# Gates of a PEER layer: float32 one-hots from one VectorE instruction, and one float32 product a token

## The chip, the cores and the metric

One Trainium2 chip, one core of it. The metric is the device time of one execution in microseconds (us): the median of several runs. Engines in the profile: PE is TensorE (PEld its weight loads), DVE is VectorE, ACT is ScalarE, POOL is GpSimd, SP is SyncE, which issues most of the DMAs.

## The reference

Two layers (`DEPTH = 2`) on 512 tokens of width 1024. Each layer is a token mixer (four heads of differential attention and eight heads of stick-breaking attention) and then PEER, a retrieval over 128² = 16384 experts of one neuron each; a residual with a factor and a layer norm follow each half. The part that matters here:

```python
q = (xt @ w_query).reshape(T, PEER_HEADS, 2, HALF_Q)
scores = einsum('thpc,hpnc->thpn', q, sub_keys)
top_s, top_i = top_k(scores, 16)
cand_s = top_s[:, :, 0, :, None] + top_s[:, :, 1, None, :]
cand_i = top_i[:, :, 0, :, None] * 128 + top_i[:, :, 1, None, :]
best_s, best_pos = top_k(cand_s, 16)
idx = take_along_axis(cand_i, best_pos)      # 8 heads x 16 = 128 experts a token
gate = softmax(best_s)
...
act = gelu(einsum('cd,ced->ce', x, expert_u[idx]))
y = einsum('ce,ced->cd', gate * act, expert_v[idx])
```

## The kernel before

The 512 tokens are four blocks of 128. PEER is done in two ways at once. For blocks 0 and 1 (`BLK_A`) the rows of the chosen experts are gathered: in each layer and block 128 rows of `u` and 128 of `v`, each by an indirect DMA that GpSimd issues (line 624), into one of five buffers named `row`, and each used by one VectorE instruction of 128x1024 (line 634 for `u`, line 645 for `v`). For blocks 2 and 3 (`BLK_B`) the function `dense` multiplies with all 16384 experts in 32 chunks of 512 on TensorE: `first` makes gelu(h·u) of a chunk, `weigh` transposes it and multiplies it with a dense matrix of gates, `second` multiplies with `v` (lines 821 to 824). Seven chunks of `first` may run ahead; the rest waits until the gates of both blocks lie in DRAM.

The function `gates` makes that dense matrix. `select` finds the 128 experts of a token and their gates; the numbers are split into a high part i and a low part j of 7 bits each (lines 667 to 672), and i, j and the gate are turned by TensorE so that the 128 choices lie on the partitions and the tokens along the row (line 675). For a token, the 128x128 matrix over (j, i) is then a product of two matrices over its 128 choices: one with a one at each choice's j, and one with its gate at each choice's i. Four tokens (`NT`) are a step, 32 steps a block, and there are two blocks and two layers, so 128 steps in all:

- `hots` compares a table of numbers (`iota_b`, bfloat16, the number repeated for four tokens) with i and with j: two 128x512 compares a step (line 700 on VectorE, or five instructions of lines 696 and 698 on ScalarE). The gate was split into three bfloat16 parts beforehand (lines 679 to 687), and the one-hot of i is multiplied with each: three 128x512 multiplies a step (line 711 on VectorE or GpSimd, or four instructions of line 709 on ScalarE). `pick` takes the engine that would end the piece first by the planner's costs.
- `products` makes 12 matmuls a step, three parts for each of four tokens (line 723), ScalarE copies the sums to a staging tile (line 727), and every 32 tokens SP stores them to DRAM (line 731).

All of `hots`' tiles come from a pool of 18 named `d2`.

The order of instructions comes from a planner inside the kernel. Threads (`early`, `rest` with `dense`, `heads`, `mixer_out`, `indices`, `gathers`, `gates`) tell before each step what it costs on each engine and how long it takes (`cost(lat, ...)`). Of the threads whose step can start within 5 us of the first one, that with the lowest time at which it is ready, less a lead of its own, is taken; `gates` has a lead of 6, `gathers` of 0. A step starts when the engines that it names are free, and its planned start becomes the priority under which the compiler orders instructions. A row step names VectorE, GpSimd and DMA and takes 2.2 us; a step of `gates` names ScalarE and TensorE, and the engines of the picks are booked besides.

Of the kernel before, what the change touches and what calls it, by code (L numbers as in the profile page):

```python
# [18 lines left out]
P = 128  # L19
# [16 lines left out]
# Pairs (a, b) of ranks that can be among the 16 best sums: (a + 1) * (b + 1) <= 16.  # L36
ROWS = [(0, 1, 16), (1, 1, 8), (2, 1, 5), (3, 1, 4), (4, 1, 3), (5, 3, 2), (8, 8, 1)]
NCAND = sum(n * m for _, n, m in ROWS)
# Token blocks whose experts are gathered row by row (A); the others (B) go through
# products with all experts, in chunks of EC, weighted by a dense matrix of gates.  # L40
# [12 lines left out]
def trunk(ctx: ExitStack, tc: tile.TileContext, x, w_in, lam, subln_g, w_o, ln1, ln2,  # L53
# [38 lines left out]
    # The order of the instructions. Threads are generators that tell, before each step that  # L92
    # they emit, how long it will hold the engines; the step that can start first is next.
# [7 lines left out]
    def pick(**engines):  # L101
        """The engine that would end a piece of work first."""
        eng = min(engines, key=lambda e: free[e] + engines[e])
        free[eng] += engines[eng]
        return eng
# [33 lines left out]
    # constants  # L139
    ident = const.tile([P, P], F32, name="ident")  # L140
    make_identity(nc, ident)
    # minus the distance of a query from a key; no weight where the key is later
# [18 lines left out]
    iota_b = const.tile([P, P, NT], BF16, name="iota_b")  # L161
    nc.gpsimd.iota(iota_b, pattern=[[1, P], [0, NT]], base=0, channel_multiplier=0,
# [4 lines left out]
    hs = {}          # a block's h: an SBUF tile (A) or an AP in DRAM (B)  # L167
# [7 lines left out]
    def load_h(b):  # L175
        """A block's h in SBUF, in a tile that may be overwritten."""
        if b in on_chip:
            return hs[b]
        t = hap.tile([P, D], F32, name="ha") if b in BLK_A else t4()
        nc.sync.dma_start(t, hs[b])  # L180
        if b in BLK_A:
            hs[b] = t
            on_chip.add(b)
        return t
# [32 lines left out]
    def layer_params(l):  # L217
# [12 lines left out]
        # -(e1 - e2 + li)  # L230
# [18 lines left out]
    def pipeline(items, stages, skew, c):  # L249
        """Emits the stages of each item, stage k of an item skew[k] steps behind its first."""  # L250
# [8 lines left out]
    def attention(l, b, q, mixT):  # L259
        """mixT[feature, t] of a block from its queries and all keys up to it."""  # L260
# [135 lines left out]
        # heads of one parity share a tile: the others' keys lie on other partitions  # L396
# [17 lines left out]
    def mixer(l, blks, order, tails):  # L414
        """Token mixer and first norm of some blocks, and their queries and key scores."""
# [9 lines left out]
        # dq dk dv sq sk sv  # L425
        for n, key in ((1, "dk"), (2, "dv"), (0, "dq"), (4, "sk"), (5, "sv"), (3, "sq")):
            o = int(key[0] == "s")
            for b in blks:
# [12 lines left out]
                else:  # L441
# [6 lines left out]
                    else:  # L448
                        # scores in units of the head's slope, a power of two
# [18 lines left out]
    def mixer_out(l, tail, hq):  # L468
# [49 lines left out]
        for b in tail:  # L518
            if b in BLK_B:
                # exact parts of h for the products with all experts  # L520
# [6 lines left out]
    def best16(rows, val, pos):  # L527
        """The 16 largest of each row, and their positions; the rows are overwritten."""
# [12 lines left out]
    def select(l, b, half, idf, gate):  # L541
        """Expert numbers (as floats) and gates of half of a block's heads: [t, head, rank]."""
# [31 lines left out]
        for h in range(HH + 1):  # L574
            yield cost(DVE=1.35, POOL=1.9)
            if h < HH:
                # a one at the position of each rank, times the expert's number
# [33 lines left out]
    def gathers(l, b):  # L611
        """y = sum over the selected experts of gate * gelu(h . u) * v, rows gathered."""
# [44 lines left out]
    def gates(l, b):  # L657
        """Dense gates of a block to DRAM: gdram[l][j, t // GT, i, t % GT] of expert i * 128 + j."""
# [7 lines left out]
        yield cost(lat=3.0, DVE=2.0, PE=0.7)  # L666
# [9 lines left out]
        t0, t1 = a2(), a2()  # L676
        gp, ij = fold(t0[:, :3 * P], 3), fold(t0[:, 3 * P:].bitcast(BF16), 2)
        ijf, gb = fold(t1[:, :2 * P], 2), fold(t1[:, 2 * P:2 * P + 3 * P // 2].bitcast(BF16), 3)
        nc.vector.tensor_copy(ij.rearrange("p a t -> p (a t)"), pt[:, 0:2 * P])
        nc.scalar.copy(ijf.rearrange("p a t -> p (a t)"), pt[:, 0:2 * P])  # L680
        # three parts of a gate, exact in bfloat16
        nc.vector.tensor_copy(gp[:, 0, :], pt[:, 2 * P:3 * P])
        for k in range(3):
            nc.vector.tensor_copy(gb[:, k, :], gp[:, k, :])
            if k < 2:
                nc.vector.tensor_sub(gp[:, k + 1, :], gp[:, k, :], gb[:, k, :])
                nc.vector.tensor_copy(gp[:, k, :], gb[:, k, :])
        shp = [P, P, NT]

        def hots(tg, t0):  # L690
            t = tg * GT + t0
            hot = a2h().rearrange("p (a j t) -> p a j t", a=2, t=NT)
            for n in range(2):
                if pick(ACT=1.7, DVE=0.34) == "ACT":
                    for k in range(NT):
                        nc.scalar.activation(hot[:, n, :, k], iota_b[:, :, k], AF.Abs, scale=-1.0,
                                             bias=ijf[:, n, t + k:t + k + 1])
                    nc.scalar.activation(hot[:, n], hot[:, n], AF.Relu, scale=-1.0, bias=1.0)
                else:
                    nc.vector.tensor_tensor(hot[:, n], iota_b, ij[:, n, t:t + NT].unsqueeze(1).to_broadcast(shp),  # L700
                                            op=ALU.is_equal)
            w01 = a2h().rearrange("p (a j t) -> p a j t", a=2, t=NT)
            w2 = a2h()[:, :P * NT].rearrange("p (j t) -> p j t", t=NT)
            ws = (w01[:, 0], w01[:, 1], w2)
# [212 lines left out]
```

## Time and profile before

| | |
|---|---|
| time, median of 3 runs | 3537.8 us (3537.52 to 3541.9) |
| span of the profiled execution, first to last instruction | 3535.5 us |
| VectorE busy | 2937.8 us (83%) |
| TensorE busy | 2765.6 us (78%) |
| GpSimd busy | 1681.0 us (48%) |
| ScalarE busy | 1184.8 us (34%) |
| moved by DMA | 1032.89 MB, 292 GB/s |

The profile is of one execution. No time from outside is given for it; its span lies 2.3 us below the median of the runs. Busy time is the time in which an engine had at least one instruction in work, so two that overlap at their ends count once; a mean or a middle (median) of a group is that of single instructions, from start to end. A matmul's end is modelled, so a busy TensorE is not one at its peak.

### The profile page before, as it was taken

What the parts mean: (1) busy time and instruction counts of PE and PEld (TensorE: products, weight loads), DVE (VectorE), ACT (ScalarE), POOL (GpSimd) and SP (SyncE); (2) the same over time, 40 slices, a digit from 0 to 9 for tenths busy, and PEclk for the clock granted to TensorE, in tenths of its full rate; (3) what the DMA queues carried; (4) which work ended last, traced back from release to release, by engine and by line L of the source; (5) the groups of instructions that cost most, each with busy time, mean ns of one, the idle gap of its engine ahead of it and who ended that gap; (6) DMA issues with size and microseconds to landing.
All of it is one profiled execution on the core that took longest, in us unless ns stands there. A gap on an engine that the chain in (4) does not pass through costs nothing.

```text
span 3535.5 us, 42200 instructions
## 1 busy us (share of the span) xinstructions
PE 2765.6 (78%) x14604; PEld 2214.2 (63%) x14604; DVE 2937.8 (83%) x5537; ACT 1184.8 (34%) x1900; POOL 1681.0 (48%) x1297
## 2 busy tenths in 40 slices
PE   7996474468576999999997876834694679999997
PEld 5776462366245888888776764613652468888885
DVE  2577889989998888888668678999799987888888
ACT  2114640411133444444231138404110434444442
POOL 0265645763675433334314655457536743344443
PEclk9997587579777999999998886865796689999998
DMA  5698796686769999999966987955966799999996
GB/s 228 212 329 294 246 333 201 206 302 231 261 222 360 360 347 343 349 351 348 369 222 253 331 286 237 351 177 196 337 220 232 256 367 343 349 346 354 345 344 251
DMA packets 283926, 1032.89 MB, mean 292 GB/s; under 512 B 25152, under 2 KB 91200, under 8 KB 231488
## 3 DMA queue, kind: packets, MB, share of 16 engines
q0 software_dynamic: 147456, 536.94, 42.4%
q1 hardware_dynamic: 136256, 493.26, 37.6%
q8 instruction: 115, 1.88, 0.2%
q14 instruction: 99, 0.81, 0.1%
HBM read 991.30 MB, written 38.80 MB: 291 GB/s over the span
## 4 chain that ended last, share of the span: by engine, by line
PE 40%; DVE 14%; issue 6%; DMA 5%; POOL 2%; ACT 2%; POOLq 0%; DVEq 0%; ACTq 0%
PE ps L822 7%; PE ps L821 7%; PE ps L824 6%; PE ps L786 5%; PE ps L785 5%; PE ps L784 5%; DVE row L634 3%; DMA row<-u,idx 2%; DVE ha L645 2%; POOL row L624 2%; DMA row<-v,idx 2%; PE ps L800 1%; DVE d L711 1%; DVE idf L586 1%; DVE d L579 1%
## 5 line engine op out<-in xcount | busy, mean ns | idle before, releaser
L624 POOL DMA_INDIRECT row<-v,idx x512 | 669.3, 1307 | 892.6 <-DVE ha L645 662.5
L624 POOL DMA_INDIRECT row<-u,idx x512 | 655.2, 1280 | 589.1 <-DVE row L634 375.9
L634 DVE SCALAR_TENSOR_TENSOR row<-row,ha 128x1024 f32<-128x1024 f32 x512 | 666.6, 1315 | 121.0 <-DMA row<-u,idx 118.1
L645 DVE SCALAR_TENSOR_TENSOR ha<-row,c,ha 128x1024 f32<-128x1024 f32 x508 | 700.3, 1379 | 58.0 <-DMA row<-v,idx 53.9
L750 DVE TENSOR_TENSOR t<-st,t 128x1024 fp32r<-128x1024 f32 x449 | 533.2, 1224 | 210.8 <-ACT t L748 210.7
L748 ACT ACTIVATE t<-st 128x1024 fp32r<-128x1024 f32 x456 | 453.9, 1056 | 36.6 <-PE ps L824 15.8
L723 PE MATMUL ps<-d,d 128*128 128x128 bf16 x1536 | 218.4, 295 | 207.0 <-DVE d L711 128.8
L821 PE MATMUL ps<-t,d 128*128 128x512 f32 x1024 | 314.2, 398 | 44.5 <-ACT d L806 44.5
L822 PE MATMUL ps<-t,d 128*128 128x512 f32 x1024 | 342.3, 395 | 0.0
L723 PEld LDWEIGHTS <-d 128*128 128x128 bf16 x1536 | 178.6, 121 | 234.5 <-issue 192.5
L824 PE MATMUL ps<-t,d 128*128 128x512 f32 x1024 | 316.7, 390 | 0.0
L785 PE MATMUL ps<-t,t 128*128 128x512 f32 x800 | 311.5, 389 | 0.5 <-DVE t L750 0.5
L786 PE MATMUL ps<-t,t 128*128 128x512 f32 x800 | 311.7, 390 | 0.0
L784 PE MATMUL ps<-t,t 128*128 128x512 f32 x800 | 304.2, 389 | 1.0 <-ACT t L748 1.0
L507 PE MATMUL ps<-t,st 128*128 128x128 f32 x2048 | 263.2, 293 | 35.2 <-DMA st<-w_query 35.2
L507 PEld LDWEIGHTS ps<-t,st 128*128 128x128 f32 x2048 | 257.8, 209 | 41.5 <-issue 29.5
L444 PE MATMUL ps<-t,st 128*128 128x128 f32 x2048 | 243.0, 281 | 22.2 <-ACT t L191 16.2
L444 PEld LDWEIGHTS ps<-t,st 128*128 128x128 f32 x2048 | 238.9, 197 | 28.6 <-ACT t L191 18.6
L821 PEld LDWEIGHTS ps<-t,d 128*128 128x128 f32 x1024 | 190.4, 190 | 82.4 <-ACT d L806 45.5
L822 PEld LDWEIGHTS ps<-t,d 128*128 128x128 f32 x1024 | 190.1, 190 | 47.0 <-DVE t L750 10.2
L824 PEld LDWEIGHTS ps<-t,d 128*128 128x128 f32 x1024 | 192.2, 188 | 40.9 <-DVE d L807 0.3
L806 ACT ACTIVATE d<-t 128x512 fp32r<-128x512 f32 x128 | 78.7, 632 | 410.9 <-DVE t L803 410.9
(175 smaller groups left out, 4190.8 us busy)
## 6 DMA issues: line engine op xcount, KB each, us to landing
st<-ut SPq DMA_DIRECT2D x128, 1024.0 KB
st<-vd SPq DMA_DIRECT2D x128, 1024.0 KB
st<-w_in SPq DMA_DIRECT2D x48, 1024.0 KB
st<-w_query SPq DMA_DIRECT2D x48, 1024.0 KB
gd<-st SPq DMA_DIRECT2D x32, 1024.0 KB
t<-gd SPq DMA_DIRECT2D x64, 512.0 KB
st<-w_o SPq DMA_DIRECT2D x24, 1024.0 KB
ln<-ln SPq DMA_DIRECT2D x16, 512.0 KB
```

The lines of the kernel that those rows point to most:

```text
L444: nc.tensor.matmul(ps[:, f * P:(f + 1) * P], lhsT=w(c, slice(f * P, (f + 1) * P)), rhs=hT[:, c, :], start=(c == 0), stop=(c == DC - 1))
L507: nc.tensor.matmul(ps[:, f * P:(f + 1) * P], lhsT=w(c, slice(f * P, (f + 1) * P)), rhs=hq[b][0][:, c, :], start=(c == 0), stop=(c == DC - 1))
L624: nc.gpsimd.indirect_dma_start(out=g, out_offset=None, in_=src, in_offset=bass.IndirectOffsetOnAxis(ap=idx[s // (NSEL // 2)][:, s % (NSEL ...
L634: nc.vector.scalar_tensor_tensor(g, g, 1.0, h1, op0=ALU.mult, op1=ALU.mult, accum_out=c[:, s:s + 1])
L645: nc.vector.scalar_tensor_tensor(y, g, c[:, s:s + 1], y, op0=ALU.mult, op1=ALU.add)
L750: (nc.gpsimd if eng == "POOL" else nc.vector).tensor_tensor(lo, part, hi.bitcast(F32), op=ALU.subtract)
L784: nc.tensor.matmul(ap[b], lhsT=xhi, rhs=hi[:, c, :], start=(d == 0), stop=False)
L785: nc.tensor.matmul(ap[b], lhsT=xhi, rhs=lo[:, c, :], start=False, stop=False)
L786: nc.tensor.matmul(ap[b], lhsT=xlo, rhs=hi[:, c, :], start=False, stop=(d == DC - 1))
L821: nc.tensor.matmul(y[b][n], lhsT=shi, rhs=hi[:, n, :], start=start, stop=False)
L822: nc.tensor.matmul(y[b][n], lhsT=shi, rhs=lo[:, n, :], start=False, stop=False)
L824: nc.tensor.matmul(y[b][n], lhsT=slo, rhs=hi[:, n, :], start=False, stop=stop)
```

## The change

The table `iota_b` becomes float32, 128 numbers, not repeated. The three-part split of the gate goes; i, j and the gate are copied out of PSUM by one ScalarE copy, in float32. For each token VectorE makes the one-hot of j by one `tensor_scalar` (compare with a number for each partition), and the gates at i by another that compares and multiplies; eight instructions of 128x128 a step, none on GpSimd or ScalarE. TensorE makes one float32 product a token instead of three in bfloat16, four matmuls a step. The planner's costs of these steps change with it. The copies to the staging tile and the stores stay. Elsewhere the diff takes out comments only.

```diff
@@ -158,13 +158,13 @@
     iota_c = const.tile([P, NCAND, TOPK], BF16, name="iota_c")
     nc.gpsimd.iota(iota_c, pattern=[[1, NCAND], [0, TOPK]], base=0, channel_multiplier=0,
                    allow_small_or_imprecise_dtypes=True)
-    iota_b = const.tile([P, P, NT], BF16, name="iota_b")
-    nc.gpsimd.iota(iota_b, pattern=[[1, P], [0, NT]], base=0, channel_multiplier=0,
+    iota_b = const.tile([P, P], F32, name="iota_b")
+    nc.gpsimd.iota(iota_b, pattern=[[1, P]], base=0, channel_multiplier=0,
                    allow_small_or_imprecise_dtypes=True)
...
@@ -663,7 +663,7 @@
         for half in range(2):
             yield from select(l, b, half, idf, gate)
         idf, gate = (t.rearrange("p h k -> p (h k)") for t in (idf, gate))
-        yield cost(lat=3.0, DVE=2.0, PE=0.7)
+        yield cost(lat=3.0, DVE=1.2, PE=0.7, ACT=0.4)
         ii = a2(I32)[:, :2 * NSEL].rearrange("p (a k) -> p a k", a=2)
         nc.vector.tensor_copy(ii[:, 1, :], idf)
         nc.vector.tensor_single_scalar(ii[:, 0, :], ii[:, 1, :], 7, op=ALU.arith_shift_right)
...
@@ -673,55 +673,28 @@
         pt = psum()
         for n, src in enumerate((fi[:, 0, :], fi[:, 1, :], gate)):
             nc.tensor.transpose(pt[:, n * P:(n + 1) * P], src, ident)
-        t0, t1 = a2(), a2()
-        gp, ij = fold(t0[:, :3 * P], 3), fold(t0[:, 3 * P:].bitcast(BF16), 2)
-        ijf, gb = fold(t1[:, :2 * P], 2), fold(t1[:, 2 * P:2 * P + 3 * P // 2].bitcast(BF16), 3)
-        nc.vector.tensor_copy(ij.rearrange("p a t -> p (a t)"), pt[:, 0:2 * P])
-        nc.scalar.copy(ijf.rearrange("p a t -> p (a t)"), pt[:, 0:2 * P])
-        # three parts of a gate, exact in bfloat16
-        nc.vector.tensor_copy(gp[:, 0, :], pt[:, 2 * P:3 * P])
-        for k in range(3):
-            nc.vector.tensor_copy(gb[:, k, :], gp[:, k, :])
-            if k < 2:
-                nc.vector.tensor_sub(gp[:, k + 1, :], gp[:, k, :], gb[:, k, :])
-                nc.vector.tensor_copy(gp[:, k, :], gb[:, k, :])
-        shp = [P, P, NT]
-
-        def hots(tg, t0):
-            t = tg * GT + t0
-            hot = a2h().rearrange("p (a j t) -> p a j t", a=2, t=NT)
-            for n in range(2):
-                if pick(ACT=1.7, DVE=0.34) == "ACT":
-                    for k in range(NT):
-                        nc.scalar.activation(hot[:, n, :, k], iota_b[:, :, k], AF.Abs, scale=-1.0,
-                                             bias=ijf[:, n, t + k:t + k + 1])
-                    nc.scalar.activation(hot[:, n], hot[:, n], AF.Relu, scale=-1.0, bias=1.0)
-                else:
-                    nc.vector.tensor_tensor(hot[:, n], iota_b, ij[:, n, t:t + NT].unsqueeze(1).to_broadcast(shp),
-                                            op=ALU.is_equal)
-            w01 = a2h().rearrange("p (a j t) -> p a j t", a=2, t=NT)
-            w2 = a2h()[:, :P * NT].rearrange("p (j t) -> p j t", t=NT)
-            ws = (w01[:, 0], w01[:, 1], w2)
-            for k, w in enumerate(ws):
-                eng = pick(ACT=1.2, POOL=1.0, DVE=0.34)
-                if eng == "ACT":
-                    for n in range(NT):
-                        nc.scalar.activation(w[:, :, n], hot[:, 0, :, n], AF.Copy, scale=gp[:, k, t + n:t + n + 1])
-                else:
-                    (nc.gpsimd if eng == "POOL" else nc.vector).tensor_tensor(
-                        w, hot[:, 0], gb[:, k, t:t + NT].unsqueeze(1).to_broadcast(shp), op=ALU.mult)
-            return hot, ws
+        ijg = fold(a2()[:, :3 * P], 3)
+        nc.scalar.copy(ijg.rearrange("p a t -> p (a t)"), pt[:, :3 * P])
+
+        def hots(t):
+
+
+            hot, w = (fold(a2(), NT) for _ in range(2))
+            for k in range(NT):
+                nc.vector.tensor_scalar(hot[:, k, :], iota_b, ijg[:, 1, t + k:t + k + 1], None, op0=ALU.is_equal)
+                nc.vector.tensor_scalar(w[:, k, :], iota_b, ijg[:, 0, t + k:t + k + 1],
+                                        ijg[:, 2, t + k:t + k + 1], op0=ALU.is_equal, op1=ALU.mult)
+            return hot, w
 
         stg = {}
 
-        def products(tg, t0, hot, ws):
+        def products(tg, t0, hot, w):
             if t0 == 0:
                 stg[tg] = [fold(st_tile().rearrange("p c f -> p (c f)"), 64) for _ in range(2)]
             ps = psum()
             for n in range(NT):
-                for k, w in enumerate(ws):
-                    nc.tensor.matmul(ps[:, n * P:(n + 1) * P], lhsT=hot[:, 1, :, n], rhs=w[:, :, n],
-                                     start=(k == 0), stop=(k == 2))
+                nc.tensor.matmul(ps[:, n * P:(n + 1) * P], lhsT=hot[:, n, :], rhs=w[:, n, :],
+                                 start=True, stop=True)
             ps = fold(ps, NT)
             for a in range(2):
                 nc.scalar.copy(stg[tg][a][:, :, t0:t0 + NT].rearrange("p i t -> p t i"),
...
@@ -733,15 +706,15 @@
 
         todo = []
         for t in range(0, P, NT):
-            yield cost(lat=0.7, ACT=0.55, PE=0.8)
-            todo.append((t // GT, t % GT, *hots(t // GT, t % GT)))
+            yield cost(lat=1.6, DVE=1.6, ACT=0.9, PE=1.0)
+            todo.append((t // GT, t % GT, *hots(t)))
             if len(todo) > 1:
                 products(*todo.pop(0))
         products(*todo.pop(0))
         done[f"gates {l} {b}"] = done["gates"] = clock[0]
```

## Rows read from the trace of the kernel before

**Rows 1.** The page's forty equal slices, busy tenths of VectorE.

```profile
DVE  2577889989998888888668678999799987888888
```

**Rows 2.** Stretches within the loops over all experts: busy us of each engine.

```profile
core 0: us, PE busy (x) PEld busy (x) DVE busy (x) ACT busy (x) POOL busy (x), PEclk, DMA share, GB/s
1150.00:1690.00 540.00, 540.00 (x2473) 445.95 (x2472) 447.70 (x468) 235.31 (x283) 210.92 (x145) 1.00 0.93 347
```

**Rows 3.** The same columns for the four stretches in which gates are made.

```profile
605.00:795.00 190.00, 104.74 (x699) 90.03 (x699) 172.95 (x215) 55.91 (x124) 134.39 (x113) 0.66 0.73 254
948.00:1097.00 149.00, 89.58 (x467) 62.02 (x467) 139.41 (x235) 47.41 (x97) 108.07 (x89) 0.67 0.72 254
2363.00:2545.00 182.00, 103.06 (x683) 87.97 (x684) 162.06 (x220) 54.54 (x123) 126.74 (x107) 0.65 0.72 253
2703.00:2837.00 134.00, 88.46 (x467) 61.33 (x467) 125.47 (x214) 44.97 (x95) 100.97 (x83) 0.71 0.70 250
```

**Rows 4.** The chain of waits at the second loop's start: start us, us, what.

```profile
2842.99 11.97 DMA t<-gd
```

**Rows 5.** Groups by line, VectorE, the row instructions in G1 to G4 in turn.

```profile
L645 DVE SCALAR_TENSOR_TENSOR ha<-row,c,ha 128x1024 f32<-128x1024 f32 x67 | 106.5, 1590 | 16.9 <-DMA row<-v,idx 16.1 <-issue 0.2
...
L634 DVE SCALAR_TENSOR_TENSOR row<-row,ha 128x1024 f32<-128x1024 f32 x51 | 73.7, 1464 | 9.6 <-DMA row<-u,idx 9.5
...
L645 DVE SCALAR_TENSOR_TENSOR ha<-row,c,ha 128x1024 f32<-128x1024 f32 x59 | 95.7, 1622 | 19.9 <-DMA row<-v,idx 19.0
...
L634 DVE SCALAR_TENSOR_TENSOR row<-row,ha 128x1024 f32<-128x1024 f32 x45 | 64.6, 1458 | 8.5 <-DMA row<-u,idx 8.5
```

**Rows 6.** Single lines, 612 to 790 and 950 to 1097 us: ns least/middle/most.

```profile
L645 DVE SCALAR_TENSOR_TENSOR ha<-row,c,ha x61: 1265/1285/3415, 612.3 to 790.0; 128x1024 f32<-128x1024 f32 x61
...
L634 DVE SCALAR_TENSOR_TENSOR row<-row,ha x50: 1205/1218/2425, 950.6 to 1093.5; 128x1024 f32<-128x1024 f32 x50
```

**Rows 7.** Groups by line, whole span: compares and multiplies; busy us, mean ns.

```profile
L711 POOL TENSOR_TENSOR d<-d,d 128x512 bf16<-128x512 bf16 x166 | 196.7, 1197 | 26.8 <-DVE d L700 23.4 <-PE ps L776 1.1 <-PE ps L723 0.5
...
L700 DVE TENSOR_TENSOR d<-iota_b,d 128x512 bf16<-128x512 bf16 x245 | 130.2, 569 | 0.0
L711 DVE TENSOR_TENSOR d<-d,d 128x512 bf16<-128x512 bf16 x195 | 123.6, 662 | 0.1
```

**Rows 8.** Timeline, G4: two multiplies and two compares in a row.

```profile
2799.31 0.75 DVE L711 TENSOR_TENSOR d<-d,d 128x512 bf16<-128x512 bf16 x2
...
2799.98 0.75 DVE L700 TENSOR_TENSOR d<-iota_b,d 128x512 bf16<-128x512 bf16 x2
```

**Rows 9.** Timeline, G3: VectorE and GpSimd from 2399 us.

```profile
2399.79 4.88 DVE L205 TENSOR_SCALAR ha<-ha,ln_mv,ln_rs 128x1024 f32<-128x1024 f32 x1
2400.08 4.03 POOL L711 TENSOR_TENSOR d<-d,d 128x512 bf16<-128x512 bf16 x4
```

**Rows 10.** Timeline of VectorE: tensor_scalar with one pointer, and what follows.

```profile
2181.84 0.28 DVE L296 TENSOR_SCALAR dg<-ident,rc 128x128 f32<-128x128 f32 x1
2182.04 0.75 DVE L643 TENSOR_SCALAR ha<-row,c 128x1024 f32<-128x1024 f32 x1
2182.70 0.28 DVE L351 TENSOR_TENSOR d<-d,neg_s 128x128 f32<-128x128 f32 x1
```

**Rows 11.** Timeline of VectorE: tensor_scalar with two pointers, and what follows.

```profile
850.74 0.79 DVE L205 TENSOR_SCALAR ha<-ha,aln_mv,aln_rs 128x1024 f32<-128x1024 f32 x1
851.45 0.08 DVE L539 MATCH_VALUE_LOAD d<-d,t 128x8 f32 x1
```

**Rows 12.** Timeline: a row issue, with two tensor_scalar beginning inside it.

```profile
257.43 0.95 POOL L624 DMA_INDIRECT row<-u,idx  x1 [0.30 <-issue]
...
258.04 0.47 DVE L296 TENSOR_SCALAR dg<-ident,rc 128x128 f32<-128x128 f32 x2
```

**Rows 13.** Chain of waits (float32 products), timeline (bfloat16 products), G3 and G4.

```profile
2505.76 4.36 PE ps L507 x20
...
2799.77 5.72 PE L723 MATMUL ps<-d,d 128*128 128x128 bf16 x46 [2.22 <-DVE d L711]
```

**Rows 14.** One line, 1700 to 1900 us: rows left after the first loop.

```profile
L645 DVE SCALAR_TENSOR_TENSOR ha<-row,c,ha x22: 1264/1285/1286, 1698.9 to 1766.8; 128x1024 f32<-128x1024 f32 x22
```

## The prediction

> **What bounds the kernel now.** I read the page's forty slices first, for the engine that stays full [rows 1]: VectorE is above 0.8 almost everywhere. Then the same sums for longer stretches, because the bound changes from one to the next. In the two loops over all experts TensorE is busy from end to end and VectorE for 83% [rows 2]; less VectorE work there buys nothing. Before each of these loops, in both layers, lie two stretches in which a block's gates are made, four in all: G1 605 to 795, G2 948 to 1097, G3 2363 to 2545, G4 2703 to 2837 us. In these VectorE is busy for 172.95 + 139.41 + 162.06 + 125.47 = 599.9 of 655 us, a share of 0.916, while TensorE stands at 386, ScalarE at 203 and GpSimd at 470 us [rows 3]. So here VectorE sets the pace. That the end of this work is waited for is seen in the chain: at the head of the second loop it stands for 11.97 us on the load of the gates that G4 has just written [rows 4]. VectorE time saved in the four stretches is thus an earlier loop, and the loops are full of TensorE work that moves with it.
>
> What fills VectorE there? Two kinds of work in turn: rows of the gathered blocks, 67 + 51 + 59 + 45 = 222 of them, and the gates' compares and multiplies. The rows are slow in these stretches: 1590, 1464, 1622 and 1458 ns on average [rows 5], where the middle one of the same lines in (nearly) the same stretches takes 1285 and 1218 [rows 6]. The compares and multiplies too: 569 and 662 ns on average [rows 7], against 415 of an undisturbed one (two in 0.75, of which the second starts 0.335 after the first) [rows 8]. The timeline shows why: one line-205 instruction on VectorE lasts 4.88 us, and within it GpSimd runs four of its line-711 multiplies, 4.03 us [rows 9]; alone the same instruction takes 0.79 [rows 11]. GpSimd's multiplies hold VectorE up.
>
> **The change, part by part.** All in VectorE time over the four stretches, 128 steps of four tokens.
>
> *Removed, compares and multiplies on VectorE:* 245 + 195 = 440 instructions [rows 7]. In a run they follow each other by (2799.98 − 2799.31) / 2 = 0.335 us [rows 8]: 147 us.
>
> *Removed, GpSimd's 166 multiplies:* they go with 196.7 us of GpSimd's time [rows 7], which counts for nothing by itself. What counts is the hold-up: 245 × (569 − 415) = 37.7 and 195 × (662 − 415) = 48.2 us for the gates' own instructions; for the rows 67 × 305 + 51 × 246 + 59 × 337 + 45 × 240 = 63.6; and 4.1 for the line-205 one. Together 154 us, 0.93 a multiply. The bounds are 0, were the hold-up from something else, and all 197 us; I take the 154 that is counted.
>
> *Removed, small work of lines 679 to 687:* nine short VectorE instructions a block, 36, at the 0.20 us of a 128-element one [rows 10]: 7 us.
>
> *Added, 1024 tensor_scalar instructions on VectorE:* of 128 float32 elements, half of them with one pointer scalar, half with two. The nearest row is line 296, one pointer, same size: the next instruction starts 0.20 us after it [rows 10]. For the second pointer: line 205 (two) holds 0.71 us [rows 11], line 643 (one, same 1024 elements) 0.66 [rows 10], so 0.05 more. 512 × 0.20 + 512 × 0.25 = 230 us. From below, 0.19 for all of them [rows 12]: 195. From above, a compare that takes one element a cycle where line 643 and line 296 show (0.66 − 0.20) / 896 = 0.51 ns an element: 0.066 more each, 298. I take 230, since line 205 shows that two operations and two pointers keep that rate.
>
> The Trainium skill, "VectorE: DVE Perf Modes", section "The TRN2 errata", speaks against such edits: a fixed cost per instruction, so tiles of at least 512 elements. By its formula with 58 cycles an instruction here would be an estimated 0.127 us and all 1024 would be 130; by the rows they are 230, so the small size is dearer than the page's figure, and the sum goes by the rows.
>
> *TensorE:* 12 bfloat16 products a step become 4 float32 ones. 46 of the old take 5.72 us, 0.124 each, 1.49 a step; 20 float32 ones of the same size take 4.36, 0.218 each where the granted clock is 0.65 on average (G3, [rows 3]), 0.87 a step [rows 13]. Gain 0.6 a step, counted as nothing: TensorE waits here for VectorE and GpSimd. If it did not wait, it would be worth up to 79 us.
>
> *ScalarE:* lines 696, 698 and 709 go, one copy becomes a little wider. It is busy for 203 of 655 us [rows 3], and its copies of line 727 remain: nothing.
>
> *Buffers, queues:* two d2 tiles a step in place of three; same stores of the gates on SP, same row issues on GpSimd, which has more room. Nothing moves past a queue by itself. But the planner's costs change: a gates step now names VectorE with 1.6 and takes a latency of 1.6 where it named 0.55 of ScalarE and took 0.7, and the picks are gone. That can turn the order of rows against gates; it is a rival below.
>
> *Sum:* 147 + 154 + 7 − 230 = 78 us of VectorE time. Of it I count the share in which VectorE is busy there, 0.916: 71 us. The trace's own time is its span of 3535.5 us, with 2.3 us to the median of the runs, 3537.8, taken as what lies around it. 3537.8 − 71 = **3466 us**, 2.0% faster. (About 0.2% is what a measurement of this kernel tells from no change.)
>
> **The rivals.**
>
> *The compare runs at one element a cycle.* Then 298 in place of 230: 10 us of VectorE time are left, 9 of the end: 3528. For it: no row shows a compare of float32 with a scalar. Against: line 700 is a compare, and at 0.335 us for 512 elements it runs faster than the rows' 1.2 us for 1024.
>
> *Something else paces two of the stretches.* In G1 and G3 other blocks' projections run on TensorE beside the gates, and their weights come while the rows do. If only half of the 71 us gets through, 3502. For it: VectorE has 8% idle there. Against: that is all the idle there is [rows 3].
>
> *Slower, by the order.* A row thread's lead is 0, the gates' is 6, and both now start from the time at which VectorE is free; a row's latency is 2.2, a step's 1.6. So the planner may put several steps between two rows where now 222 rows stand to 128 steps. What is pushed out of G1 and G2 must end before block 1 can enter layer 1. In the loop DMA is 0.93 busy already [rows 2], so rows can be pushed past it, and there a row takes (1766.8 − 1698.9) / 21 = 3.23 us [rows 14], while in G1 or G2 it took 1.285 / 0.916 = 1.40. Each such row loses 1.83; it decides from 71 / 1.83 = 39 of the 118 rows of G1 and G2. With 60 it is 3466 + 110 = 3576. Against: VectorE is idle for 17% of the loop, so part of the rows will fit, and a row that only moves into the loop costs nothing.
>
> *Slower, by the port.* The new instructions could shut row issues out: eight in a run are 1.8 us a step, 230 us over all. If each delays the rows that VectorE waits for next, the time is 3466 + 0.916 × 230 = 3677; it ends slower than before from a third of that on. Against: an issue of 0.95 us runs across two line-296 instructions, which keep their 0.19 us [rows 12], and five row buffers lie between.
> The Trainium skill, "SBUF — State Buffer", section "Who interferes with whom", says that VectorE in a two-port mode and GpSimd shut each other out for the whole instruction; with GpSimd's multiplies the trace agrees (the 4.88 us), with its row issues it does not show it.
>
> **How the numbers follow.** The forecast 0.58; the slow compare 0.10; the half gain 0.14; the order 0.12; the port 0.06. Low end: if every microsecond of GpSimd's 197 was hold-up and all instructions take 0.19, the VectorE gain is 147 + 197 + 7 − 195 = 156, with the share 143: 3395; I take 3400. High end 3545: it takes in the slow compare and half of the orders that lose something; left out are the port, an order with many late rows and a still larger gain, under 2 in 10. Faster by over 0.2%: the forecast, nearly all of the half gain, over half of the slow compare, 0.76. Within 0.2%: 0.07. Slower: 0.17.
>
> **What would show it.** Right: tensor_scalar rows that follow each other by 0.20 to 0.25 us; the row lines back at 1285 and 1218 ns in the gates' stretches; GpSimd with row issues alone there; TensorE's loops as long as now but begun earlier by about half of the 71 us in layer 0 and by all of it in layer 1. Wrong: tensor_scalar at over 0.27; rows after the end of the first loop at 3 us each with block 1 late; row issues that last as long as the runs of tensor_scalar; or stretches whose VectorE share falls well under 0.9, with another engine waited for.

## The result, and the profile after

The changed kernel takes 3473.7 us (3469.36 to 3479.05, 4 runs) against 3537.7 (3535.67 to 3541.9, 4 runs) of the kernel before beside it: a ratio of 0.9821, 95% interval 0.9804 to 0.9837. That is 64 us, where 71 were forecast. The profiled execution has a span of 3470.1 us, 65.4 less than before.

First the page of the changed kernel: busy time of the engines, and the line of VectorE in the forty slices that answers to [rows 1].

```profile
PE 2726.6 (79%) x14092; PEld 2169.2 (63%) x14092; DVE 2861.2 (82%) x6083; ACT 1142.3 (33%) x1757; POOL 1473.9 (42%) x1133
...
DVE  2577889889998888888579678898899888888887
```

VectorE worked for 2937.8 us and works for 2861.2: 76.6 less, where the sum said 78. The span is VectorE's busy time and its idle time together, so the 65.4 us are 76.6 of work gone and 11.2 of idle time more (597.7 before, 608.9 now). This split is used for every run below.

The groups by line (busy us, mean ns, idle before): first the rows in the kernel before, then in the changed one the rows, the products and the two new instructions.

```profile
L645 DVE SCALAR_TENSOR_TENSOR ha<-row,c,ha 128x1024 f32<-128x1024 f32 x508 | 700.3, 1379 | 58.0 <-DMA row<-v,idx 53.9 <-DVE ha L645 0.2 <-issue 0.2
L634 DVE SCALAR_TENSOR_TENSOR row<-row,ha 128x1024 f32<-128x1024 f32 x512 | 666.6, 1315 | 121.0 <-DMA row<-u,idx 118.1 <-issue 1.4
```

```profile
L645 DVE SCALAR_TENSOR_TENSOR ha<-row,c,ha 128x1024 f32<-128x1024 f32 x508 | 656.3, 1292 | 90.8 <-DMA row<-v,idx 85.3 <-DVE ha L645 0.6 <-issue 0.3
L634 DVE SCALAR_TENSOR_TENSOR row<-row,ha 128x1024 f32<-128x1024 f32 x512 | 648.3, 1281 | 105.0 <-DMA row<-u,idx 101.4 <-issue 1.9
L696 PE MATMUL ps<-d,d 128*128 128x128 f32 x1024 | 192.7, 311 | 19.6 <-DVE d L685 16.0
L685 DVE TENSOR_SCALAR d<-iota_b,d 128x128 f32<-128x128 f32 x512 | 185.0, 361 | 0.0
L684 DVE TENSOR_SCALAR d<-iota_b,d 128x128 f32<-128x128 f32 x512 | 148.5, 290 | 0.0
```

Over the whole span the rows' means were 1379 and 1315 ns before and are 1292 and 1281 now, within some 5% of the middle ones in [rows 6]. Together the two lines take 62.3 us less (44.0 and 18.3). How the new instructions follow each other is seen in the timeline (start us, us):

```profile
2705.85 0.29 DVE L684 TENSOR_SCALAR d<-iota_b,d 128x128 f32<-128x128 f32 x1
2706.05 0.35 DVE L685 TENSOR_SCALAR d<-iota_b,d 128x128 f32<-128x128 f32 x1
2706.30 0.29 DVE L684 TENSOR_SCALAR d<-iota_b,d 128x128 f32<-128x128 f32 x1
```

By 0.20 and 0.25 us: 512 pairs of 0.45 are the 230 us of the sum.

Where the time went is read from stretches cut at the starts and ends of the loops over all experts (columns as in [rows 2]). First the kernel before, then the changed one, from 600 us on:

```profile
600.00:1107.00 507.00, 303.92 (x1622) 221.86 (x1622) 472.88 (x1004) 123.72 (x252) 316.95 (x259) 0.72 0.71 251
1107.00:1820.00 713.00, 706.50 (x3332) 581.86 (x3333) 575.63 (x654) 305.67 (x393) 268.11 (x184) 0.99 0.92 346
...
2856.00:3513.00 657.00, 653.14 (x2975) 539.13 (x2976) 550.71 (x583) 283.38 (x340) 266.94 (x175) 0.99 0.93 347
3513.00:3535.00 22.00, 0.56 (x3) 0.14 (x1) 18.27 (x27) 0.00 (x0) 3.07 (x3) 0.62 0.23 96
```

```profile
600.00:1020.00 420.00, 280.46 (x1366) 196.98 (x1366) 390.28 (x1206) 100.46 (x180) 173.11 (x138) 0.84 0.71 258
1020.00:1733.00 713.00, 704.87 (x3306) 579.76 (x3307) 563.66 (x667) 295.50 (x378) 290.06 (x197) 0.99 0.94 354
...
2731.00:3388.00 657.00, 653.69 (x2974) 539.60 (x2975) 549.18 (x612) 283.25 (x339) 262.39 (x179) 0.99 0.92 346
3388.00:3470.00 82.00, 0.68 (x3) 0.21 (x2) 64.79 (x63) 0.00 (x0) 42.20 (x36) 0.54 0.75 258
```

The loops are as long as before, 713 and 657 us, and begin 87 us earlier in the first layer and 125 earlier in the second. Of these 125, 60 are given back: 82 us follow the last product and not 22. In them block 1 still gathers its last rows:

```profile
L645 DVE SCALAR_TENSOR_TENSOR ha<-row,c,ha x39: 1232/1285/1321, 3384.4 to 3458.0; 128x1024 f32<-128x1024 f32 x39
```

So the order of work has changed too. Counted in VectorE's order of instructions, 332 and 845 rows stood ahead of the first weighing of the two loops before, and 2 behind the last loop; now it is 296, 811 and 38. Between 942 and 1001 us, the pure gates of the second stretch, VectorE is busy for 59.00 of 59 us and hardly a row issue is left on GpSimd:

```profile
942.00:1001.00 59.00, 56.95 (x270) 40.67 (x271) 59.00 (x259) 32.73 (x62) 1.58 (x2) 0.96 0.46 176
```

Two theories stand from here on. **Hold-up:** the gain is VectorE time, above all that which GpSimd's multiplies took from it; the order only shifts things. **Order:** the gain is that steps of gates come ahead of rows, so that the loops begin earlier and rows fill them.

### The profile page after: what moved, and what is told of

It is laid out like the page before. It is cut to its first block, busy times and chain, and to the rows that moved or that the text cites. A ratio compares the mean times of both kernels' runs of the same rounds, so it can differ in the third digit from the quotient of the medians.

```text
span 3470.1 us, 41243 instructions
## 1 busy us (share of the span) xinstructions
PE 2726.6 (79%) x14092; PEld 2169.2 (63%) x14092; DVE 2861.2 (82%) x6083; ACT 1142.3 (33%) x1757; POOL 1473.9 (42%) x1133
## 4 chain that ended last, share of the span: by engine, by line
PE 39%; DVE 11%; issue 7%; DMA 7%; POOL 4%; ACT 2%; POOLq 0%; SPq 0%; DVEq 0%; ACTq 0%
PE ps L795 6%; PE ps L794 6%; PE ps L797 6%; PE ps L759 5%; PE ps L758 5%; PE ps L757 5%; POOL row L624 3%; DMA row<-v,idx 2%; DVE row L634 2%; DMA row<-u,idx 2%; PE ps L696 2%; PE ps L773 1%; DVE ha L645 1%; DVE idf L586 1%; PE ps L507 1%
## 5 line engine op out<-in xcount | busy, mean ns | idle before, releaser
L624 POOL DMA_INDIRECT row<-v,idx x512 | 654.5, 1278 | 897.1 <-DVE ha L645 586.3
L624 POOL DMA_INDIRECT row<-u,idx x512 | 664.8, 1298 | 839.0 <-DVE row L634 608.9
L634 DVE SCALAR_TENSOR_TENSOR row<-row,ha 128x1024 f32<-128x1024 f32 x512 | 648.3, 1281 | 105.0 <-DMA row<-u,idx 101.4
L645 DVE SCALAR_TENSOR_TENSOR ha<-row,c,ha 128x1024 f32<-128x1024 f32 x508 | 656.3, 1292 | 90.8 <-DMA row<-v,idx 85.3
L749 PE MATMUL ps<-st,t 128*128 128x512 f32 x448 | 200.9, 607 | 10.5 <-DMA st<-ut 10.5
L696 PE MATMUL ps<-d,d 128*128 128x128 f32 x1024 | 192.7, 311 | 19.6 <-DVE d L685 16.0
```

The source lines that it names most:

```text
L624: nc.gpsimd.indirect_dma_start(out=g, out_offset=None, in_=src, in_offset=bass.IndirectOffsetOnAxis(ap=idx[s // (NSEL // 2)][:, s % (NSEL ...
L634: nc.vector.scalar_tensor_tensor(g, g, 1.0, h1, op0=ALU.mult, op1=ALU.mult, accum_out=c[:, s:s + 1])
L645: nc.vector.scalar_tensor_tensor(y, g, c[:, s:s + 1], y, op0=ALU.mult, op1=ALU.add)
```

## Experiments

Each of the twelve ran beside the kernel before on the same chip. The table gives the median, the ratio with its interval, the rows ahead of the two loops and behind the last, and of the profiled execution VectorE's busy and idle time. The profiled executions of e1 and e5 were the slowest of their runs, both 6.6 us above the median. The changed kernel did not run beside these; by its ratio it would take 3477 (0.9821 of about 3540).

| kernel | us | ratio | rows | busy | idle |
|---|---|---|---|---|---|
| before | 3540 | 1 | 332, 845, 2 | 2937.8 | 597.7 |
| changed | 3474 | 0.9821 [0.9804, 0.9837] | 296, 811, 38 | 2861.2 | 608.9 |
| e1 before, no multiply on GpSimd | 3551.3 | 1.0022 [1.0013, 1.0032] | 378, 889, 0 | 2825.2 | 730.9 |
| e2 bfloat16, all on VectorE | 3598.5 | 1.0158 [1.0140, 1.0175] | 380, 888, 0 | 2848.4 | 747.0 |
| e3 changed + free GpSimd multiplies | 3500.6 | 0.9879 [0.9860, 0.9899] | 291, 806, 43 | 2903.5 | 594.9 |
| e4 changed, bfloat16 tiles | 3486.4 | 0.9846 [0.9821, 0.9872] | 291, 812, 38 | 2867.7 | 616.3 |
| e5 changed, lead 3 | 3503.0 | 0.9887 [0.9864, 0.9910] | 331, 858, 0 | 2870.2 | 637.7 |
| e6 changed, lead 4 | 3510.4 | 0.9918 [0.9891, 0.9944] | 311, 832, 17 | 2860.9 | 645.1 |
| e7 changed, lead 0 | 3535.2 | 0.9981 [0.9968, 0.9994] | 345, 892, 0 | 2867.3 | 667.3 |
| e8 changed + GpSimd multiply in the step | 3606.3 | 1.0182 [1.0158, 1.0205] | 295, 804, 44 | 2985.8 | 614.2 |
| e9 = e1, rows held | 3511.6 | 0.9915 [0.9902, 0.9928] | 307, 817, 31 | 2826.6 | 683.4 |
| e10 = before, rows held | 3540.4 | 0.9994 [0.9983, 1.0005] | 308, 820, 28 | 2935.3 | 599.4 |
| e11 = e2, rows held | 3489.8 | 0.9854 [0.9840, 0.9869] | 306, 818, 31 | 2856.1 | 631.6 |
| e12 changed, old planner costs | 3485.7 | 0.9848 [0.9832, 0.9864] | 263, 790, 57 | 2865.1 | 616.6 |

**e1, the hold-up taken away alone.**

```diff
-                eng = pick(ACT=1.2, POOL=1.0, DVE=0.34)
+                eng = pick(ACT=1.2, DVE=0.34)
```

> The kernel before, with the multiplies of line 711 on VectorE or ScalarE only; nothing else. If GpSimd's multiplies cost VectorE the 154 us of hold-up that was counted, then 154 goes and at most 166 x 0.335 = 56 us comes: 98 us of VectorE time less, times 0.916 is 90, so 3448. In VectorE's order, though, 378 and 889 rows now stand before the two loops over all experts where 332 and 845 stood, and the loops have room for rows on VectorE: if a row moved ahead of a loop is lost time (1.40 us each), 44 of them give 62 back and it is 3510. If GpSimd's share was a relief to VectorE and no hold-up, 56 us of work come without a return and it is slower: 3590. The row instructions should fall back to 1285 and 1218 ns in the gates' stretches by the first, stay near 1600 and 1460 by the last.

The hold-up went: the groups by line have the compares and multiplies at 414 and 419 ns (569 and 662 in [rows 7]), the rows at 1283.

```profile
L645 DVE SCALAR_TENSOR_TENSOR ha<-row,c,ha 128x1024 f32<-128x1024 f32 x508 | 652.0, 1283 | 51.0 <-DMA row<-v,idx 48.9 <-DVE d L711 0.3
L634 DVE SCALAR_TENSOR_TENSOR row<-row,ha 128x1024 f32<-128x1024 f32 x512 | 650.0, 1283 | 142.0 <-DMA row<-u,idx 140.4
L711 DVE TENSOR_TENSOR d<-d,d 128x512 bf16<-128x512 bf16 x326 | 121.7, 419 | 1.5 <-ACT d L698 1.3
L700 DVE TENSOR_TENSOR d<-iota_b,d 128x512 bf16<-128x512 bf16 x248 | 93.1, 414 | 0.0
```

VectorE worked 113 us less than before, 36 less than in the changed kernel, and the time did not fall; none of the three times expected came. The stretches of e1 show where it stayed:

```profile
600.00:1118.00 518.00, 298.45 (x1622) 216.08 (x1622) 467.16 (x1162) 145.38 (x316) 300.36 (x223) 0.71 0.83 293
1118.00:1629.00 511.00, 510.53 (x2333) 421.78 (x2334) 425.40 (x417) 227.25 (x272) 206.65 (x130) 1.00 0.93 350
1629.00:1842.00 213.00, 208.87 (x1052) 166.06 (x1051) 101.87 (x150) 82.33 (x127) 23.75 (x11) 1.00 0.60 217
...
3404.00:3541.00 137.00, 136.87 (x625) 112.55 (x624) 76.95 (x83) 55.11 (x68) 3.84 (x2) 1.00 0.53 187
```

The written order put 46 and 44 more rows ahead of the loops; the first begins 11 us later than before. Block 1's rows are then done at 1629 us, and in the last 213 us of the first loop and 137 of the second DMA falls from 0.93 to 0.60 and 0.53 and VectorE stands idle for 111 and 60 us. So read, the time saved was spent on rows that the loop would have taken in for nothing; e9 and e11 try that.

**e2, all bfloat16 work on VectorE.** Compares and multiplies all go to VectorE, and the planner's costs are those of the change.

```diff
-                if pick(ACT=1.7, DVE=0.34) == "ACT":
+                if False:
...
-                eng = pick(ACT=1.2, POOL=1.0, DVE=0.34)
+                eng = "DVE"
...
-            yield cost(lat=0.7, ACT=0.55, PE=0.8)
+            yield cost(lat=1.6, DVE=1.6, ACT=0.9, PE=1.0)
```

> The kernel before, with all compares and multiplies on VectorE in bfloat16 (five instructions of 128x512 a step, three products a token), and the planner's costs of the changed kernel for a step. VectorE: 154 us of hold-up gone, 640 - 440 = 200 instructions x 0.335 = 67 us more, 87 less in all, times 0.916 is 80: 3458 if only the sum of VectorE's work counts. 380 and 888 rows stand before the loops where 332 and 845 stood: with 1.40 us each for 43 rows 60 of that is given back, 3518. If the float32 form itself (one product, eight small instructions) is what pays, it stays at the time before, 3538, or above.

It is 1.6% slower than before, with 89 us less work on VectorE and 149 us more idle time. Of what was expected only the last came by its time (3538 or above); its reason, that the float32 form itself is what pays, does not hold: this kernel's VectorE work, 2848.4 us, is below the changed kernel's 2861.2, and e11 takes most of the loss away without that form. The order is that of e1, though the planner's costs are the change's, so these costs alone don't make the changed kernel's order.

**e3, GpSimd multiplies added.** One multiply of a constant 128x512 tile a step, 128 in all; its output is not read.

```diff
+            nc.gpsimd.tensor_tensor(jo[t // NT % 2], jk, jk, op=ALU.mult)
```

> The changed kernel, with one more GpSimd multiply of 128x512 bfloat16 in each of the 128 steps, whose result nobody reads. If a GpSimd multiply holds VectorE up by 0.93 us, 119 us come back on VectorE, times 0.916 is 109: 3583. If GpSimd's work is harmless to VectorE, 3474. If what matters is that GpSimd issues the rows later, the idle time before the row instructions for DMA grows and their own length stays.

Some 24 us came (3500.6 against 3477), between the two, and it tells neither: having no input that a step makes, all 128 ran in the first 182 us (the line's instructions: least/middle/most ns, first and last start).

```profile
L690 POOL TENSOR_TENSOR jo<-jk x128: 1029/1038/2017, 3.5 to 182.4; 128x512 bf16<-128x512 bf16 x128
```

**e4, bfloat16 tiles in the changed kernel.** The tiles `hot` and `w` are bfloat16, so a token is one bfloat16 product; the gates are rounded to bfloat16 in it, which the reference doesn't do.

```diff
-            hot, w = (fold(a2(), NT) for _ in range(2))
+            hot, w = (fold(a2h()[:, :512], NT) for _ in range(2))
```

> The changed kernel with the one-hot and the weighted one-hot written in bfloat16: one bfloat16 product a token, gates rounded (the two lower parts of a gate are left out). TensorE has half the passes or less, VectorE the same 1024 instructions. If VectorE alone paces the gates' steps, 3474 within 10. If the float32 product paces them too (TensorE stands at 48.5 of 50 us in G2 of the changed kernel), the two stretches G2 and G4 get shorter and it is 3450 to 3465.

TensorE worked 73 us less (2653.3) and the time is not shorter, so TensorE's products don't pace the steps.

**e5 to e7, the order alone.** The changed kernel with another lead of the gates' thread; no instruction is added or taken away. For e5:

```diff
-                        spawn(gates(l, b), 6.0)
+                        spawn(gates(l, b), 3.0)
```

> The changed kernel with the lead of the gates' thread cut from 6 to 3, so that the written order again puts as many rows ahead of the expert loops as the kernel before did (331 and 858 VectorE rows ahead of them against 296 and 811 in the changed kernel, 332 and 845 before; none left at the end). If only the VectorE work removed counts and its order does not, the time stays at the changed kernel's, 3474 us (3464 to 3484). If the place of the rows counts, the second layer's loop starts 47 rows x about 1.4 us = 66 us later than 2731, thus at 2797, and the end loses its row tail (82 down to 23 us): 2797 + 657 + 23 = 3477 us, the same time by another way, with loops that start at about 1070 and 2797. Rival: with the steps squeezed between rows again VectorE waits for each row's transfer as it did not in the changed kernel, and the time goes to 3510 or more.

> As the run before it with a lead of 4: 311 and 832 rows ahead of the loops, 17 left at the end. If the order does not count: 3474 us (3464 to 3484). If it does: the loop starts 21 rows x 1.4 = 29 us later than 2731, at 2760, and about 17 of 38 tail rows are left (23 + 17/38 x 59 = 49 us): 2760 + 657 + 49 = 3466 us. Rival: a row moved ahead costs more than the 1.4 us, then the time is over 3480.

> The changed kernel with no lead of the gates' thread: 345 and 892 rows ahead of the loops, none left at the end: as many as the kernel before with all its bf16 work on VectorE or without GpSimd multiplies had. If only VectorE's work counts: 3474 us (3464 to 3484), as the instructions are the same. If the place of the rows counts: the loop of the second layer starts 81 rows x 1.4 = 113 us later than 2731, at 2844, and with 657 of loop and 23 of tail the end is at 3524 us (3505 to 3545), most of the gain gone with no instruction added.

The order counts, by more than expected in e5 and e6. With before's order (e5) the change is worth 37 us and not 64; with 892 rows ahead (e7) 5 us are left. VectorE's work is the same within 10 us in the changed kernel and these three; its idle time rises from 608.9 to 637.7, 645.1 and 667.3. In e7 the second loop shows the picture of e1, rows done 153 us before its end:

```profile
2867.00:3365.00 498.00, 498.00 (x2277) 411.53 (x2278) 415.84 (x409) 219.51 (x262) 208.28 (x129) 1.00 0.94 351
3365.00:3518.00 153.00, 152.83 (x698) 125.50 (x697) 84.24 (x91) 63.70 (x78) 1.48 (x1) 1.00 0.53 191
```

Not all that e7 loses need come from the rows: its first loop lasts 836 us and not 713, with 3693 matmuls and not 3306 in it; 256 of the others are line 507, a projection of the next layer.

A fixed price of a row ahead of the loop doesn't fit, though: e6 has fewer rows ahead than e5, loops that are full to their ends, and is no faster. Its extra 36 us of idle time against the changed kernel are spread over the stretches ahead of the loops, waits for row transfers among them; why this order waits more is open.

**e8, the multiply where the hold-up would be.** As e3, but the multiply reads the step's one-hot and so can't run ahead of it; its output is not read.

```diff
+            nc.gpsimd.tensor_tensor(jo[t // NT % 2], hot.rearrange("p a t -> p (a t)"), jk, op=ALU.mult)
```

> The changed kernel with one GpSimd multiply of 128x512 a step that reads the step's one-hot tile, so that it can't run ahead of its step (its output is not read): 128 multiplies, 295 and 804 rows ahead of the loops, nearly the changed kernel's order. If a GpSimd multiply holds VectorE up by 0.93 us as in the kernel before: 128 x 0.93 x 0.916 = 109 us more, 3583 us (3550 to 3600). If it holds VectorE up only where both want the same instant and most of it falls beside stalls: 3500 us, as with the multiplies that had no place of their own. If GpSimd does not hold VectorE up at all: 3474 us, the row issues behind the multiplies being hidden.

The hold-up theory's 109 us were expected and some 129 came (3606.3 against 3477), 1.0 us for each of the 128: VectorE's busy time grows by 124.6, its idle time by 5. The timeline of e8 shows one of them:

```profile
1035.69 0.27 DVE L687 TENSOR_SCALAR d<-iota_b,d 128x128 f32<-128x128 f32 x1
1035.89 0.33 DVE L688 TENSOR_SCALAR d<-iota_b,d 128x128 f32<-128x128 f32 x1
1036.11 1.20 POOL L690 TENSOR_TENSOR jo<-d,jk 128x512 bf16<-128x512 f32 x1 [1.58 <-DVE d L687]
1036.14 1.25 DVE L687 TENSOR_SCALAR d<-iota_b,d 128x128 f32<-128x128 f32 x1
1037.31 0.34 DVE L688 TENSOR_SCALAR d<-iota_b,d 128x128 f32<-128x128 f32 x1
```

A compare of 0.27 us that begins 0.03 after the multiply lasts 1.25, and the next one starts at 1037.31, where the multiply ends. The Trainium skill, "SBUF — State Buffer", section "Who interferes with whom", has this as a rule for a VectorE instruction in a two-port mode: of VectorE and GpSimd the one that comes first keeps the shared ports for its whole instruction. The trace agrees (1.25 us in place of 0.27); in which mode the compare runs, it does not show.

**e9 to e11, the order held by hand.** In the kernels of e1, of before and of e2, block 1's rows from the 41st `u` row on wait for a one-element mark that VectorE writes at the last step of each gates thread. That gives 306 to 308 and 817 to 820 rows ahead, near the changed kernel's.

```diff
+            if b == 1 and s == 40:
+                for n in BLK_B:
+                    yield f"gates {l} {n}"
+                    nc.vector.tensor_copy(c[:, s:], marks[l, n].to_broadcast([P, NSEL - s]))
...
+        marks[l, b] = sel.tile([P, 1], F32, name="mark")
+        nc.vector.tensor_copy(marks[l, b], todo[0][3][0][:, 127, NT - 1:])
```

> The kernel of the first run (before without multiplies on GpSimd), with the rows of block 1 held back: from its 41st u row on they wait for a one-element mark that VectorE writes at the last step of each gates thread, so that 307 and 817 rows stand ahead of the loops and not 378 and 889 (296 and 811 in the changed kernel). If the order was what kept the first run from gaining, this one gains: VectorE worked 36 us less there than in the changed kernel (2825 against 2861), times 0.916 = 33, and 6 to 11 rows more ahead of the loops cost about 8: 3474 + 8 - 33 = 3449 us (3430 to 3470). Rival: bf16 steps with twelve products can't run one behind the other as the changed kernel's steps do, then VectorE idles in them and the time stays at 3510 to 3560.

> The kernel before with the same hold on block 1's rows: 308 and 820 rows ahead of the loops and not 332 and 845; its arithmetic is unchanged, GpSimd multiplies included. The changed kernel lost 29 us when its order went back from 296 and 811 to 331 and 858; if the order is worth that by itself, about 25 rows of 47 give 15 to 20 us: 3523 us (3508 to 3535). Rival: with GpSimd's multiplies in the steps the steps can't run alone any faster, rows that were interleaved with them were free, and the time is 3541 us or more.

> The kernel of the second run (all bf16 compares and multiplies on VectorE) with the same hold: 306 and 818 rows ahead and not 380 and 888. If the order alone made that run slower than the kernel before (3598): VectorE's 2848 us against the changed kernel's 2861 times 0.916 = 12 less, the rows 8 more: 3470 us (3450 to 3495). Rival: the bf16 steps themselves are slow (their products on TensorE or the copies behind them), then 3540 to 3600 us.

e10 shows no gain from the order by itself: with GpSimd's multiplies in place the loops begin earlier (1077 and 2810 us), the rows behind the last one take 68 us, and the end is where it was. e11 shows the other half: e2's instructions, in an order near the change's, fall from 3598.5 to 3489.8. VectorE's work is the same within 8 us, 115 us of idle time are gone, and rows fill the loops to their ends (DMA 0.94 and 0.93):

```profile
1041.00:1755.00 714.00, 704.05 (x3311) 579.48 (x3312) 577.25 (x666) 295.11 (x378) 298.64 (x198) 0.99 0.94 354
...
2758.00:3415.00 657.00, 653.52 (x2972) 539.62 (x2973) 548.96 (x605) 283.80 (x340) 249.13 (x178) 0.99 0.93 346
```

That is within 13 us of the changed kernel, with no float32 one-hot and no float32 product in it. So about 51 of the 64 us come without the float32 form; the other 13 are that form's or what is left of a difference in order.

e9 gained 40 us on e1, but not the expected 100: its idle time stays at 683.4, and its 3511.6 lie in the range of the rival named before it ran, steps that wait. Two waits of VectorE stand in its trace that e11 has not (us in total, times, longest): a multiply for products of TensorE, and the mark itself for a tile that ScalarE makes, which is a cost of the hold.

```profile
DVE d L715 <- PE ps L727: 23.4, 20, 4.7
DVE mark L745 <- ACT d L713: 16.2, 2, 8.1
```

They are 40 of the 52 us of idle time that e9 has more than e11. Its first loop lasts 759 us (1050 to 1809) and not 713; what holds it was not tried.

**e12, fewer rows ahead.** The changed kernel with the old costs in the planner.

```diff
-            yield cost(lat=1.6, DVE=1.6, ACT=0.9, PE=1.0)
+            yield cost(lat=0.7, ACT=0.55, PE=0.8)
...
+            pick(DVE=1.6)
```

> The changed kernel with the planner's old costs of a step (ACT 0.55, PE 0.8, latency 0.7, and 1.6 booked on VectorE within the step): 263 and 790 rows ahead of the loops, 57 left at the end and not 38. If fewer rows ahead go on to help: the second loop starts 21 rows x about 2 us = 42 us earlier and 19 more rows x 1.9 = 36 us follow it: 3474 - 42 + 36 = 3468 us (3455 to 3485). Rival: the best order is passed, the rows behind the loop cost all that the earlier start gains and more: 3490 us or above.

The second loop begins 21 us earlier (2710), and 116 us follow it in place of 82. The time is 3485.7, no better than the changed kernel's; the intervals of the two ratios just overlap. No run beat the changed kernel.

## Why the prediction was right, and where its steps were not

*The sum* held. The changed kernel takes 76.6 us from VectorE where 147 + 154 + 7 − 230 = 78 were worked out. Its parts show where the gain lies: the rows' two lines give back 62.3 us, where 63.6 were counted, while the new instructions take with 230 about what the old ones took with their hold-up, 147 + 37.7 + 48.2 = 233. Most of the gain on VectorE is the hold-up of other work, not a cheaper way to make the tiles. Its least certain term, the hold-up of 0.93 us for each GpSimd multiply, measured 0.97 a multiply in e8 (124.6 / 128; that multiply reads float32 and lasts a little longer, 1.35 us on average against 1.20 in [rows 7]). The price of the new instructions, bounded by 0.19 and, for the dearer kind, 0.32, was 0.20 and 0.25 as taken; the rival of a slow compare falls. The small work of lines 679 to 687 was not tried alone.

*The step from VectorE time to the end* was incomplete: "VectorE time saved in the four stretches is thus an earlier loop". e1 saved more of it and ended no earlier. It is true only if the time is not at once filled with rows that the loop could hold. The two orders make a square, in medians beside the kernel before: in about before's order the new arithmetic is worth 37 us (e5), in about the change's order 63 (from e10's 3540.4 to 3477). The order alone is worth nothing with the old arithmetic (ratio 0.9994) and 26 us with the new. Neither theory stands alone: the work had to go and the rows had to stay for the loops, and some 40% of the gain needed an order that the prediction had only as a danger. The orders are alike by their counts of rows only, and e6 shows that these counts don't fix the time. The prediction did not work out which order the planner's new costs would give, and e7, with the same instructions in another order, keeps 5 us of the gain: that the time came within 7 us of the forecast was in part luck.

*The place* was off. Expected were loops that begin earlier by about half of 71 us in layer 0 and by all of it in layer 1; they begin 87 and 125 earlier, and 60 return behind the last loop. The rival "slower by the order" had this mechanism, but in layer 0, at 3.23 us a row behind the loop, and with nothing gained by rows taken from the stretches ahead. In layer 0 the rows do end 47 us later (1814.4 against 1766.8), yet block 0's first row of layer 1 comes 43 earlier (1860.4 against 1903.6). At the end of layer 1 a row costs (3458.0 − 3384.4) / 38 = 1.94 us. The mechanism came and its price didn't.

*TensorE* was mis-sized: "4 float32 ones, 0.87 a step". A float32 product stands in the trace as two matmuls, 1024 for 512 products, so the 20 of [rows 13] were ten products, and at their 0.218 us each a step of eight takes 1.74, no gain on the 1.49 of before. In the changed kernel (columns as in [rows 2]) the second run of gates begins at the lower clock (a share of 0.50, 1.2 GHz), 15 matmuls in 3 us. Then the clock stands at 1.00, and they come no faster than VectorE makes the tiles, which has no idle time: 46 in 10 us, 1.74 us a step again.

```profile
943.00:946.00 3.00, 3.00 (x15) 2.99 (x14) 3.00 (x14) 1.06 (x2) 0.88 (x1) 0.50 0.95 322
960.00:970.00 10.00, 9.67 (x46) 6.59 (x45) 10.00 (x45) 5.71 (x12) 0.00 (x0) 1.00 0.35 140
```

The gain was counted as nothing, and e4 shows that rightly: with half the matmuls the time is no shorter.

*The port* rival falls: row issues last 1278 and 1298 ns on average and lasted 1307 and 1280. These averages alone say little, since in the new order only 32 of the 1024 issues meet the new instructions at all; but the 30 that run across several of them last 0.95 us in the middle, those that meet none 1.02. One of them (start us, us):

```profile
2652.76 0.94 POOL L624 DMA_INDIRECT row<-u,idx  x1 [0.31 <-DVE d L685]
2652.94 0.27 DVE L684 TENSOR_SCALAR d<-iota_b,d 128x128 f32<-128x128 f32 x1
2653.13 0.33 DVE L685 TENSOR_SCALAR d<-iota_b,d 128x128 f32<-128x128 f32 x1
```

*Half the gain* did not come: of the 76.6 us of work 65.4 reached the end, and 11.2 went into idle time.

Open are why the bfloat16 kernels' own order puts 46 rows more ahead of the loops, what e6's order waits for, e9's longer first loop, and what makes up the 13 us between e11 and the changed kernel.

## What to carry to other kernels

Price GpSimd work beside a full VectorE by what it takes from VectorE, here 0.93 and 0.97 us for a multiply of 1.20 and 1.35 on average, and not by GpSimd's own idle time. Time saved ahead of a stage that another engine bounds is worth something only if the work that could hide in that stage is still there to fill it: look at DMA and VectorE in the last part of the stage, and hold such work back if it is done early. Splitting the span into busy and idle time of the engine that bounds tells at once which of the two an edit has changed.

## What the runs showed of the hardware

A higher granted TensorE clock came with the float32 products and bought no time in these steps. The same stretch of the changed kernel and of e4, with one bfloat16 product a token, in turn:

```profile
870.00:1001.00 131.00, 82.11 (x330) 51.62 (x329) 129.45 (x448) 36.81 (x69) 46.94 (x37) 0.82 0.56 196
```

```profile
870.00:1001.00 131.00, 63.72 (x206) 27.97 (x204) 127.58 (x443) 39.91 (x74) 42.62 (x33) 0.63 0.52 188
```

The clock, a mean over its levels of 2.4 and 1.2 GHz, is 0.82 against 0.63 of the upper one, with TensorE busy for 82 against 64 us; VectorE is busy for 129 and 128 of 131 us, and the time is no shorter for it. A 128-element tensor_scalar with a second pointer scalar and a second operation costs 0.05 us more than one with the first alone, the same as on 1024 elements [rows 10, 11].
